# A two-layer conditioned trunk on one core: adaLN sums 1024 columns wide on VectorE, rope in three operations, wider splits and a new instruction list

## The chip, the core and the metric

The kernel runs on 1 core of one Trainium2 chip. The engines are TensorE (PE; its weight loads are listed apart as PEld), VectorE (DVE), ScalarE (ACT), GpSimd (POOL) and SyncE (SP, which issues most transfers). The metric is device time of one execution in microseconds (us), here the median of 3 runs. A profile is taken from one further execution of the same program.

## What is computed

Batch 1, 256 tokens, width 1024, two layers, fp32. Layer 0 is "even" (sliding-window heads A with sinks, beside heads B with compressed, selected and window keys), layer 1 is "odd" (16 heads, block attention).

```python
c_act = silu(c)
for layer in range(2):
    ada = c_act @ w_ada[layer] + b_ada[layer]      # 1024 -> 3 * 1024
    shift, scale, gate = split(ada, 3)
    h = rms_norm(x, norm_g[layer]) * (1 + scale) + shift
    y = even_mixer(h, ...) if layer == 0 else odd_mixer(h, ...)
    x = x + gate * y
return rms_norm(x, final_g)

def even_mixer(h):   # one input projection, two head groups, silu gate paths, one output projection
    oa = sliding_window(rope(q_a), rope(k_a), v_a, sinks) * silu(z_a)
    k_cmp, v_cmp = gelu((blocks + pe) @ w1) @ w2   # compressed keys and values: 15 blocks of 32 tokens
    ob = gates of (attention to k_cmp, to selected blocks, to a window) * silu(z_b)
    return concat(oa, ob) @ w_out
```

Shortened here; rope turns the two halves of each 64-wide head against each other: (x1 cos - x2 sin, x2 cos + x1 sin).

## The kernel before

Weights come from HBM once, as tiles `raw` of 128 x 2048 (a ring of `RAW` = 5). PE multiplies in a rounded form of fp32: a number is split into a rounded high half (`whi`, made by ACT) and the rest (`wlo`, a subtraction on DVE), and `mm3` makes three matmuls of the halves. `split` does so in pieces of `spl` columns; `SPL` holds that width for layer 0's attention, its out projection, and two parts of layer 1. The activations' halves are `hhi`, `hlo` (the input of a layer) and `ghi`, `glo` (the input of an out projection). Rings give `whi` and `wlo` four tiles each.

The adaLN sums c_act @ w_ada are, apart from layer 0's shift and scale (made in the start), cut into jobs that `fill()` puts between other work: layer 0's gate (`G0_ON`), layer 1's shift and scale (`SS_ON`) and layer 1's gate (`G1_ON`). Their letters say who does them. "v": DVE multiplies 512 columns of each of the eight row blocks by a scalar per partition and adds them up in `acc` (`ada_sums`, 8 pieces); then PE adds over the 128 partitions, by a matmul with ones. "p": PE does it all, by eight matmuls 32 x 256 that stand in four column groups (`ada_rows`, tiles `raw`, `cz`), a copy `asb`, and matmuls of `asb` with `selbc` or two columns of `ta`. The tile `cz` is silu(c).

Attention is done four softmaxes at a time (`attn_four`): scores on PE into `ps_s` (two banks), mask and maximum on DVE, exp on ACT, a division by multiplying with `rc` on DVE, or on ACT for the places in `ON_ACT` (a place is n, i, t; those with t = 1 are 256 wide), then transposes on PE. `compress` makes the compressed keys (`uT` is blocks + pe, `hx` and `hg` are the gelu's, `kcbd` the keys in block-diagonal form), and `cmp_softmax` their scores and softmax.

Every call on an engine is only recorded, by `Plan.record`; all instructions therefore carry the line of `Plan.issue`, which issues them (L251 here, L246 in the changed kernel). The order is the list `ORDER`, a permutation of the recorded calls, written out in the kernel. Each engine takes its own instructions strictly in that order; between engines only semaphores wait.

The jobs of layer 0 are spread so:

```python
jobs = [lambda: gate_bias(0)] + ada_jobs(ada_gate, 0, G0_ON, 2) + ada_jobs(ada_shift_scale, 1, SS_ON, 1)
spl[0] = SPL[0]
fill(1)
gate_path(W0, 640, 0); a_quad(0); ...; compress(); cmp_softmax(); fill(1); ...; b_pair(3, True); ...
spl[0] = SPL[1]
out_proj(w_out_even[0], lambda: fill(2))
fill(len(jobs))
```

Of the kernel before, what the change touches and what calls it, by code (L numbers as in the profile page):

```python
# [1356 lines left out]
```

## Time and profile before

| | |
|---|---|
| median of 3 runs | 307.33 us (306.77 to 308.2) |
| the profiled execution's own time | 307.55 us |
| its span | 305.4 us |
| instructions | 6362 |
| granted TensorE clock | 1.00 of full speed in every stretch from 71.6 to 298.2 us, 0.86 in the last 7 us |
| bytes read from HBM | 70.38 MB |

The span runs from the first to the last recorded instruction; the profiled execution's own time is 2.2 us more than that, and 0.2 us above the median. All times below are in us from the span's start unless a duration in ns is meant. A busy time is the time in which at least one instruction of the engine is in progress; matmuls overlap, so the durations of their records add up to more than the time PE spends on them. An fp32 matmul leaves two records in the trace, a rounded one leaves one.

Rough stages: the start, with layer 0's input projection, to 71.6; layer 0's attention to about 154; its out projection and the norm and input of layer 1 to about 163; layer 1 to 298.2, where PE ends; final norm and output to 305.4.

### The profile page before, as it was taken

The page shows a single profiled execution, that of the slowest core. Times are in us where ns is not written, and L with a number is a line of the kernel's source. Part 1 is how long each engine was busy: PE and PEld are TensorE (multiplying, and loading weights), DVE is VectorE, ACT ScalarE, POOL GpSimd, SP SyncE. Part 2 cuts the span into 40 slices and gives each one's busy share as a digit, 9 for nine tenths or more (in the row PEclk, how much of TensorE's full clock was granted, in tenths as well). Part 3 has the DMA queues.
Part 4 walks back from the last instruction along what each step waited for, and adds up shares of the span by engine and source line. Part 5 has one row for each costly group of instructions (what it writes and reads, how often), then busy time and mean ns, then how long its engine had stood idle before and what let it go on. Part 6 is the DMA issues. An engine that isn't in the chain of part 4 may idle for free.

```text
span 305.4 us, 6362 instructions
## 1 busy us (share of the span) xinstructions
PE 294.5 (96%) x2331; PEld 252.0 (83%) x2331; DVE 258.4 (85%) x703; ACT 184.3 (60%) x483; POOL 11.3 (4%) x36
## 2 busy tenths in 40 slices
PE   8899999999999999999999999999999999999990
PEld 8777788997789787888877899999789989877890
DVE  1388999998899999999989778598857999997783
ACT  3476147876679778882547854264647646873630
POOL 6000000002000000000001000000000000000011
PEclk9999999999999999999999999999999999999998
DMA  8999999986956979489899292968098493151003
GB/s 240 355 364 372 387 402 372 332 261 194 337 194 197 320 260 329 139 246 339 259 274 329 61 328 63 366 206 290 0 277 276 144 298 113 52 225 71 0 9 128
DMA packets 60669, 71.82 MB, mean 235 GB/s; under 512 B 2712, under 2 KB 52320, under 8 KB 60640
## 3 DMA queue, kind: packets, MB, share of 16 engines
q1 hardware_dynamic: 60032, 70.90, 70.1%
q10 hardware_dynamic: 448, 0.48, 0.4%
q8 instruction: 18, 0.29, 0.4%
q0 software_dynamic: 160, 0.05, 0.3%
q14 instruction: 11, 0.09, 0.1%
HBM read 70.38 MB, written 1.05 MB: 234 GB/s over the span
## 4 chain that ended last, share of the span: by engine, by line
PE 84%; ACT 4%; DMA 4%; DVE 3%; issue 2%; SPq 0%; POOL 0%; POOLq 0%; ACTq 0%; DVEq 0%
PE ps_pj L251 49%; PE ps_s L251 12%; PE ps_m L251 8%; PE ps_pt L251 7%; PE ps_o L251 7%; DMA raw<-in_w_in_even_dram 2%; DMA xs<-in_x_dram 2%; ACT whi L251 2%; DVE wlo L251 1%; ACT t L251 1%; DVE xs L251 1%; DVE t L251 1%; ACT bigA L251 1%; SPq L251 0%; ACT hhi L251 0%
## 5 line engine op out<-in xcount | busy, mean ns | idle before, releaser
L251 ACT CAST whi<-raw 128x512 fp32r<-128x512 f32 (+1 forms) x132 | 74.7, 599 | 28.8 <-PE ps_pj L251 17.2
L251 DVE TENSOR_TENSOR wlo<-raw,whi 128x512 fp32r<-128x512 f32 (+1 forms) x116 | 74.0, 659 | 8.9 <-ACT whi L251 8.7
L251 PE MATMUL ps_pj<-hhi,whi 128*128 128x256 f32 x256 | 68.0, 286 | 0.0
L251 PE MATMUL ps_pj<-hhi,wlo 128*128 128x256 f32 x256 | 67.8, 286 | 0.0
L251 PE MATMUL ps_pj<-hlo,whi 128*128 128x256 f32 x256 | 67.3, 283 | 0.0
L251 PEld LDWEIGHTS ps_pj<-hhi,whi 128*128 128x128 f32 x256 | 46.5, 188 | 1.1 <-issue 0.3
L251 PEld LDWEIGHTS ps_pj<-hhi,wlo 128*128 128x128 f32 x256 | 46.3, 188 | 0.6 <-issue 0.3
L251 PEld LDWEIGHTS ps_pj<-hlo,whi 128*128 128x128 f32 x256 | 46.3, 188 | 0.1
L251 DVE SCALAR_TENSOR_TENSOR acc<-raw,cz,acc 128x512 f32<-128x512 f32 x42 | 31.3, 745 | 0.3
L251 ACT ACTIVATE sm<-sm,mn 128x256 f32<-128x256 f32 (+1 forms) x58 | 26.0, 450 | 6.5 <-DVE mn L251 6.4
L251 PE MATMUL ps_pj<-whi,hhi 128*128 128x512 f32 (+2 forms) x72 | 26.0, 375 | 0.8 <-ACT hhi L251 0.8
L251 DVE SCALAR_TENSOR_TENSOR wlo<-raw,whi 128x512 fp32r<-128x512 f32 x32 | 21.2, 686 | 5.1 <-ACT whi L251 5.1
L251 PE MATMUL ps_pj<-wlo,hhi 128*128 128x512 f32 (+2 forms) x72 | 25.3, 377 | 0.0
L251 PE MATMUL ps_pj<-whi,hlo 128*128 128x512 f32 (+2 forms) x72 | 25.0, 369 | 0.0
L251 PE MATMUL ps_pj<-whi,ghi 128*128 128x512 f32 (+1 forms) x56 | 20.8, 375 | 0.0
L251 PE MATMUL ps_pj<-wlo,ghi 128*128 128x512 f32 (+1 forms) x56 | 20.5, 372 | 0.0
L251 ACT COPY pT<-ps_pt 128x384 f32<-128x384 f32 x25 | 11.9, 476 | 14.2 <-PE ps_pt L251 14.2
L251 PE MATMUL ps_pj<-whi,glo 128*128 128x512 f32 (+1 forms) x56 | 20.1, 365 | 0.0
L251 PEld LDWEIGHTS ps_pj<-whi,hhi 128*128 128x128 f32 x72 | 13.4, 188 | 3.5 <-ACT hhi L251 1.4
L251 PE MATMUL ps_pt<-ta,sm 128*128 128x128 f32 x87 | 15.7, 276 | 0.0
L251 DVE TENSOR_TENSOR t<-ps_pj,tb 128x512 f32<-128x512 f32 (+2 forms) x22 | 12.0, 586 | 3.4 <-PE ps_pj L251 3.4
L251 PEld LDWEIGHTS ps_pj<-wlo,hhi 128*128 128x128 f32 x72 | 13.3, 189 | 1.9 <-DVE wlo L251 0.2
(231 smaller groups left out, 613.2 us busy)
## 6 DMA issues: line engine op xcount, KB each, us to landing
raw<-in_w_in_odd_dram SPq DMA_DIRECT2D x16, 1024.0 KB, 7.6
raw<-in_w_ada_dram SPq DMA_DIRECT2D x28, 512.0 KB, 5.7
raw<-in_w_in_even_dram SPq DMA_DIRECT2D x8, 652.0 KB, 7.0
raw<-in_w_in_even_dram SPq DMA_DIRECT2D x5, 1024.0 KB, 9.0
t<-in_w_ada_dram SPq DMA_DIRECT2D x16, 256.0 KB, 6.0
raw<-in_w_out_even_dram SPq DMA_DIRECT2D x4, 1024.0 KB, 5.4
raw<-in_w_out_odd_dram SPq DMA_DIRECT2D x4, 1024.0 KB, 6.3
qT<-in_w_ada_dram SPq DMA_DIRECT2D x12, 256.0 KB, 7.2
```

The costliest lines, as they stand in the source:

```text
L251: self.ops.append(dict(key=eng.key, deps=deps, fn=lambda: getattr(real, name)(*args, **kw)))
```

## The change

1. The adaLN jobs are all done by DVE and are 1024 columns wide: `ada_wide` makes two multiply-adds of 1024 columns for each of four tiles `raw`. Layer 0's gate is one job, layer 1's shift and scale are two (four of the eight column blocks each, shift and scale together), layer 1's gate is one. Shift and scale end in four matmuls 32 x 256 in four column groups, a copy `asb` on ACT and two transposes. Layer 1's gate (`GATE_R`) splits its sums into rounded halves, and adds over the partitions by four rounded matmuls with ones in the place of two fp32 ones.
2. Rope: the two half-wide multiplications with the sine are one, which reads the halves of each head in reverse order by a negative step. `_box`, which finds which memory a call touches, learns negative steps.
3. `compress` adds the position rows in four additions instead of eight. `cmp_softmax` holds the compressed keys still and streams the queries, in four column groups, then copies and transposes back: 4 matmuls 32 x 256, one copy, 2 transposes for 8 matmuls of 128 x 32.
4. `SPL`: splits of 1024 columns in layer 0's attention and out projection.
5. `ON_ACT`: all the 256-wide scalings of `attn_four` (layer 0) go to ACT, twelve more than before.
6. The three sets of small rows share one transpose, `hr` has one buffer instead of two, and `ORDER` is a new list.

```diff
 START = ((2, 0), (2, 4), (2, 6), (2, 6))
-SS_ON = "vvvp"
-G0_ON = "vp"
-G1_ON = "vv"
-SPL = (512, 512, 512, 512)
+GATE_R = (0, 1)
+SPL = (1024, 1024, 512, 512)
 CUT = 384
-ON_ACT = ((0, 1, 1), (1, 1, 1))
+ON_ACT = ((0, 0, 1), (0, 1, 1), (1, 0, 1), (1, 1, 1))
 T4B = 4
 SMB = 5
 BANKS = {"pj": 3, "s": 2, "pt": 1, "o": 1, "m": 1}
@@ -35,131 +33,126 @@
 INIT = 3e38
...
 
         dims = [tuple(d) for d in ap.ap]
-        p0, f0 = divmod(ap.offset, dims[0][0])
+        off = ap.offset + sum(st * (n - 1) for st, n in dims[1:] if st < 0)
+        dims = dims[:1] + [(abs(st), n) for st, n in dims[1:]]
+        p0, f0 = divmod(off, dims[0][0])
         free = tuple(d for d in dims[1:] if d[0] and d[1] > 1)
...
-    rows = const([64, P], "rows")
-    rows_pe = const([32, P], "rows_pe")
+    rows = const([96, P], "rows")
...
-        T.transpose(pr[:, :64], rows, ident[:64, :64])
-        V.tensor_copy(rT[:, :64], pr[:, :64])
+        T.transpose(pr[:, :96], rows, ident[:96, :96])
+        V.tensor_copy(rT, pr[:, :96])
...
-    def ada_tile(l, cols, spare=None):
...
+    ones_r = const([P, P], "ones_r", F32R)
+    G.tensor_copy(ones_r, ones)
+    def ada_wide(l, c0, n, u, a):
         src = w_ada[l].rearrange("(k p) n -> p k n", p=P)
+        w = sb([P, 2048], "raw", RAW).rearrange("p (k n) -> p k n", n=1024)
+        for s in range(1024 // n):
+            Y.dma_start(w[:, :, s * n : s * n + n], src[:, 2 * u : 2 * u + 2, c0 + s * D : c0 + s * D + n])
+        for k in range(2):
+            ck = cz[:, 2 * u + k, 0:1]
+            if u == 0 and k == 0:
+                V.tensor_scalar(a, w[:, k, :], ck, None, op0=ALU.mult)
             else:
+                V.scalar_tensor_tensor(a, w[:, k, :], ck, a, op0=ALU.mult, op1=ALU.add)
+    def ada_shift_scale(l, g, a):
         pa = bank("m")
+        plan.group([
+            T.matmul(pa[32 * q : 32 * q + 32, : 2 * P], ones[:, 0:32], a[:, 256 * q : 256 * q + 256], start=True, stop=True, tile_position=(0, 32 * q))
+            for q in range(4)
+        ])
         asb = sb([P, 2 * P], "asb", 2)
         A.copy(asb, pa[:, : 2 * P])
+        pc = bank("m")
+        for b in range(2):
+            T.transpose(pc[:, b * P : (b + 1) * P], asb[:, b * P : (b + 1) * P], ident)
+        pv = pc[:, : 2 * P].rearrange("p (b s j e) -> p s j b e", b=2, s=2, j=2)[:, :, :, :, 0]
+        bs = bT[:, 24 * l : 24 * l + 16].rearrange("p (s j) -> p s j", s=2)[:, :, g : g + 4].rearrange("p s (j b) -> p s j b", b=2)
+        dst = shs[:, l, :, g : g + 4]
         for s in range(2):
+            V.tensor_tensor(dst[:, s].rearrange("p (j b) -> p j b", b=2), pv[:, s], bs[:, s], ALU.add)
+        V.tensor_tensor(dst[:, 1], dst[:, 1], ngT[:, 8 * l + g : 8 * l + g + 4], ALU.mult)
+    def ada_gate(l, a):
+        if GATE_R[l]:
+            hi, lo = split(a, 1024)
+        for h in range(2):
+            pc = bank("m")
+            hs = slice(512 * h, 512 * h + 512)
+            if GATE_R[l]:
+                T.matmul(pc, ones_r, hi[:, hs], start=True, stop=False)
+                T.matmul(pc, ones_r, lo[:, hs], start=False, stop=True)
             else:
+                T.matmul(pc, ones, a[:, hs], start=True, stop=True)
+            V.tensor_tensor(gate[:, hs], pc, gate[:, hs], ALU.add)
+    def ada_jobs(l, c0, n, fin):
+        a = sb([P, 1024], "acc", 1)
+        r = [lambda u=u: ada_wide(l, c0, n, u, a) for u in range(4)]
+        last = r.pop()
+        return r + [lambda: (last(), fin(a))]
...
         V.tensor_tensor(t1, src, cs.unsqueeze(1).to_broadcast([P, n, HD]), ALU.mult)
-        V.tensor_tensor(t2[:, :, 0:32], src[:, :, 32:64], sn[:, 0:32].unsqueeze(1).to_broadcast([P, n, 32]), ALU.mult)
-        V.tensor_tensor(t2[:, :, 32:64], src[:, :, 0:32], sn[:, 32:64].unsqueeze(1).to_broadcast([P, n, 32]), ALU.mult)
+        V.tensor_tensor(
+            t2.rearrange("p h (u d) -> p h u d", u=2),
+            src.rearrange("p h (u d) -> p h u d", u=2)[:, :, ::-1, :],
+            sn.rearrange("p (u d) -> p u d", u=2).unsqueeze(1).to_broadcast([P, n, 2, 32]),
+            ALU.mult,
+        )
         dst = t1 if dst is None else dst
...
     def start_sums(g, n, d, w):
-        a = sb([P, 512], "acc", 1)
+        a = sb([P, 1024], "acc", 1)
...
-                for g in range(2):
-                    V.tensor_tensor(
-                        uT[:, 8 * hf : 8 * hf + 8, g, 0:15],
-                        src[:, :, g, :],
-                        pe.unsqueeze(2).to_broadcast([P, 8, 15]),
-                        ALU.add,
-                    )
+                V.tensor_tensor(
+                    uT[:, 8 * hf : 8 * hf + 8, :, 0:15],
+                    src,
+                    pe.unsqueeze(2).unsqueeze(3).to_broadcast([P, 8, 2, 15]),
+                    ALU.add,
+                )
...
-            hr = sb([P, 2, 4, 32], "hr", 2)
+            hr = sb([P, 2, 4, 32], "hr", 1)
...
     def cmp_softmax():
+        pa = bank("m")
+        plan.group([
+            T.matmul(pa[32 * hp_ : 32 * hp_ + 32, :S], kcbd[:, hp_ // 2, :], qbT[:, hp_, :], start=True, stop=True, tile_position=(0, 32 * hp_))
+            for hp_ in range(4)
+        ])
+        asb = sb([P, 2 * P], "asb", 2)
+        A.copy(asb, pa[:, :S])
         pc = bank("m")
         for t in range(2):
-            for hp_ in range(4):
-                T.matmul(
-                    pc[:, t * P + 32 * hp_ : t * P + 32 * hp_ + 32],
-                    qbT[:, hp_, t * P : (t + 1) * P],
-                    kcbd[:, hp_ // 2, :],
-                    start=True,
-                    stop=True,
-                )
+            T.transpose(pc[:, t * P : (t + 1) * P], asb[:, t * P : (t + 1) * P], ident)
...
-    jobs = [lambda: gate_bias(0)] + ada_jobs(ada_gate, 0, G0_ON, 2) + ada_jobs(ada_shift_scale, 1, SS_ON, 1)
+    jobs = [lambda: gate_bias(0)] + ada_jobs(0, 2 * D, 1024, lambda a: ada_gate(0, a))
+    for g_ in (0, 4):
+        jobs += ada_jobs(1, P * g_, 512, lambda a, g_=g_: ada_shift_scale(1, g_, a))
...
-    jobs += ada_jobs(ada_gate, 1, G1_ON, 2)
+    jobs += ada_jobs(1, 2 * D, 1024, lambda a: ada_gate(1, a))
```

Where layer 0's attention does adaLN sums on DVE, its instructions stood so before (an ISA row is a mask with a maximum; `sm`, `bigA` softmax tiles, `den`, `rc` their sums and reciprocals, `mn` the maxima):

```order
L251 TENSOR_SCALAR sm_125<-sm_125,rc_138 128x128
L251 TENSOR_TENSOR wlo_114<-raw_101,whi_110 128x512
L251 TENSOR_SCALAR acc_105<-raw_100,cz 128x512
L251 SCALAR_TENSOR_TENSOR acc_105<-raw_100,cz,acc_105 128x512 x2
L251 ISA sm_124,mn_134<-ps_s_90,tb 128x128
L251 ISA mn_134 128x1
L251 ISA sm_125,mn_134<-ps_s_91,tb 128x256
L251 ISA mn_134 128x1
```

On the same engine at the same place of the program the new list has:

```order
L246 TENSOR_SCALAR sm_125<-sm_125,rc_137 128x128
L246 TENSOR_TENSOR wlo_113<-raw_100,whi_109 128x1024
L246 RECIPROCAL rc_138<-den_135 128x4
L246 TENSOR_TENSOR vz<-ps_m_66,blk 128x512
L246 SCALAR_TENSOR_TENSOR acc_104<-raw_101,cz,acc_104 128x1024
L246 ISA sm_124,mn_133<-ps_s_90,tb 128x256
L246 ISA mn_133 128x1
L246 SCALAR_TENSOR_TENSOR acc_104<-raw_101,cz,acc_104 128x1024
L246 ISA sm_124,mn_133<-ps_s_90,tb 128x128
```

Between the mask operations stand pieces of 1024 columns, a subtraction and two multiply-adds, where a subtraction, a first product and two multiply-adds of 512 stood.

On PE, at the border of the layers (`ghi`, `glo` are the out projection's input, `hhi`, `hlo` layer 1's; ta with `t` is a transpose of layer 1's input), before:

```order
L251 MATMUL ps_s_91<-whi_109,glo 128x512
L251 MATMUL ps_o_96<-ta,t_86 128x128
L251 MATMUL ps_m_67<-raw_102,cz 32x256 x8
L251 MATMUL ps_pj_92<-whi_110,hhi 128x512
L251 MATMUL ps_pj_92<-wlo_114,hhi 128x512
L251 MATMUL ps_pj_92<-whi_110,hlo 128x512
L251 MATMUL ps_pj_92<-whi_110,hhi 128x512
L251 MATMUL ps_pj_92<-wlo_114,hhi 128x512
L251 MATMUL ps_m_67<-ta,asb_107 128x2
```

and in the new list, from the last matmul of the out projection:

```order
L246 MATMUL ps_s_90<-whi_108,glo 128x512
L246 MATMUL ps_pj_93<-ta,t_85 128x128 x2
L246 MATMUL ps_o_95<-ta,t_85 128x128
L246 MATMUL ps_pj_93<-ta,t_85 128x128 x2
L246 MATMUL ps_pj_91<-whi_109,hhi 128x512
L246 MATMUL ps_pj_91<-wlo_113,hhi 128x512
L246 MATMUL ps_o_95<-ta,t_85 128x128
L246 MATMUL ps_pj_93<-ta,t_88 128x128 x4
L246 MATMUL ps_pj_91<-whi_109,hlo 128x512
L246 MATMUL ps_pj_91<-whi_109,hhi 128x512
L246 MATMUL ps_o_95<-ta,t_85 128x128 x2
```

The eight matmuls of the last "p" job no longer stand ahead of layer 1's first matmul, but more of the transposes of its input stand behind it. A little further on, the second shift-and-scale job of layer 1 ends among layer 1's matmuls:

```order
L246 MATMUL ps_pj_92<-whi_109,hlo 128x512
L246 MATMUL ps_m_66<-acc_104,ones 32x256 x4
L246 MATMUL ps_pj_92<-whi_110,hhi 128x512
L246 MATMUL ps_pj_92<-wlo_114,hhi 128x512
L246 MATMUL ps_m_66<-ta,asb_105 128x128 x2
```

Its four matmuls and two transposes stand where the two-column matmuls of `ta` and `asb` stood.

More of the change, by code (lines that the diff above doesn't have):

```diff
@@ L325, in tile_trunk @@
     G.dma_start(rows[0:16, :], norm_g.rearrange("l (k p) -> (l k) p", p=P))
-    G.dma_start(rows_pe[0:16, :], cmp_pe_k.rearrange("o (i t) d -> (o i) (t d)", t=2))
-    G.dma_start(rows_pe[16:32, :], cmp_pe_v.rearrange("o (i t) d -> (o i) (t d)", t=2))
+    G.dma_start(rows[64:80, :], cmp_pe_k.rearrange("o (i t) d -> (o i) (t d)", t=2))
+    G.dma_start(rows[80:96, :], cmp_pe_v.rearrange("o (i t) d -> (o i) (t d)", t=2))
     ident = ta[:, 0:128]
@@ L365, in small_rows @@
             V.tensor_scalar(bs, bs, 1.0, None, op0=ALU.add)
-        pr = bank("pt")
-        T.transpose(pr[:, :32], rows_pe, ident[:32, :32])
-        V.tensor_copy(rT[:, 64:96], pr[:, :32])
     oT = const([P, KT, S], "oT")
@@ L404, in tile_trunk @@
     glo = const([P, KT, S], "glo", F32R)
-    def ada_tile(l, cols, spare=None):
-        if spare is None:
-            raw = sb([P, 2048], "raw", RAW)
-            spare = (raw[:, :1024], raw[:, 1024:])
+    ones_r = const([P, P], "ones_r", F32R)
+    G.tensor_copy(ones_r, ones)
+    def ada_wide(l, c0, n, u, a):
         src = w_ada[l].rearrange("(k p) n -> p k n", p=P)
-        halves = []
-        for u in range(2):
-            w = spare[u].rearrange("p (k n) -> p k n", k=4)
-            ks = slice(4 * u, 4 * u + 4)
-            if cols[1] == cols[0] + 1:
-                Y.dma_start(w, src[:, ks, cols[0] * P : (cols[0] + 2) * P])
-            else:
-                for s in range(2):
-                    Y.dma_start(w[:, :, s * P : (s + 1) * P], src[:, ks, cols[s] * P : (cols[s] + 1) * P])
-            halves.append(w)
-        return halves
@@ L424, in ada_rows @@
-    def ada_rows(w):
-        pa = bank("m")
-        for i in range(2):
-            for q in range(4):
-                k = 4 * i + q
-                T.matmul(
-                    pa[32 * q : 32 * q + 32, : 2 * P],
-                    cz[:, k, :],
-                    w[k // 4][:, k % 4, :],
-                    start=(i == 0),
-                    stop=(i == 1),
-                    tile_position=(0, 32 * q),
-                )
+        w = sb([P, 2048], "raw", RAW).rearrange("p (k n) -> p k n", n=1024)
@@ L437, in ada_rows @@
         asb = sb([P, 2 * P], "asb", 2)
         A.copy(asb, pa[:, : 2 * P])
-        return asb
-    def ada_sums(l, cols, u, a):
-        src = w_ada[l].rearrange("(k p) n -> p k n", p=P)
-        w = sb([P, 2048], "raw", RAW).rearrange("p (k n) -> p k n", n=512)
-        for s in range(2):
-            Y.dma_start(w[:, :, s * 256 : s * 256 + 256], src[:, 4 * u : 4 * u + 4, cols[s] * P : (cols[s] + 2) * P])
-        for k in range(4):
-            ck = cz[:, 4 * u + k, 0:1]
-            wk = w[:, k, :]
-            if u == 0 and k == 0:
-                V.tensor_scalar(a, wk, ck, None, op0=ALU.mult)
-            else:
-                V.scalar_tensor_tensor(a, wk, ck, a, op0=ALU.mult, op1=ALU.add)
@@ L455, in ada_shift_scale @@
-    def ada_shift_scale(l, g, n, a=None, st=None):
-        gs = slice(g, g + n)
-        bview = bT[:, 24 * l : 24 * l + 16].rearrange("p (s j) -> p s j", s=2)[:, :, gs]
-        if a is None:
-            a = ada_rows(ada_tile(l, (g, 8 + g)))
-        st = st if st is not None else ones if n == 2 else sel
-        pc = bank("m")
-        for q in range(2 * n):
-            T.matmul(pc[:, 2 * q : 2 * q + 2], a[:, q * P : (q + 1) * P], st[:, 0:2], start=True, stop=True)
-        pv = pc[:, 0 : 4 * n].rearrange("p (s j e) -> p s j e", s=2, e=2)[:, :, :, 0]
-        ng = ngT[:, 8 * l + g : 8 * l + g + n]
-        V.tensor_tensor(shs[:, l, 0, gs], pv[:, 0, :], bview[:, 0, :], ALU.add)
-        if n == 1:
-            V.scalar_tensor_tensor(shs[:, l, 1, gs], pv[:, 1, :], bview[:, 1, :], ng, op0=ALU.add, op1=ALU.mult)
-        else:
-            V.tensor_tensor(shs[:, l, 1, gs], pv[:, 1, :], bview[:, 1, :], ALU.add)
-            V.tensor_tensor(shs[:, l, 1, gs], shs[:, l, 1, gs], ng, ALU.mult)
@@ L474, in tile_trunk @@
-    selbc = const([P, P], "selbc")
-    G.tensor_copy(selbc, sel[:, 0:1].to_broadcast([P, P]))
-    def ada_gate(l, h, n, a=None):
-        pc = bank("m")
-        if n == 2:
-            T.matmul(pc, ones, a, start=True, stop=True)
-        else:
-            T.matmul(pc[:, :256], selbc, ada_rows(ada_tile(l, (16 + h, 17 + h))), start=True, stop=True)
-        gs = gate[:, h * P : (h + 2 * n) * P]
-        V.tensor_tensor(gs, pc[:, : 256 * n], gs, ALU.add)
-    def ada_jobs(fn, l, on, w):
-        r = []
-        for i, ch in enumerate(on):
-            if ch == "v":
-                c0 = 2 * i * w
-                cols = (c0, 8 + c0) if fn is ada_shift_scale else (16 + c0, 18 + c0)
-                a = sb([P, 512], "acc", 1)
-                r.append(lambda cols=cols, a=a: ada_sums(l, cols, 0, a))
-                r.append(lambda cols=cols, a=a, c0=c0: (ada_sums(l, cols, 1, a), fn(l, c0, 2, a=a)))
-            else:
-                r += [lambda i=i, j=j: fn(l, (2 * i + j) * w, 1) for j in range(2)]
-        return r
+        pc = bank("m")
@@ L715, in start_sums @@
     def start_sums(g, n, d, w):
-        a = sb([P, 512], "acc", 1)
+        a = sb([P, 1024], "acc", 1)
         av = a[:, : 256 * n].rearrange("p (s c) -> p s c", s=2)
@@ L951, in cmp_softmax @@
     def cmp_softmax():
+        pa = bank("m")
[5 more added lines that the diff above has]
+        A.copy(asb, pa[:, :S])
         pc = bank("m")
         for t in range(2):
-            for hp_ in range(4):
-                T.matmul(
-                    pc[:, t * P + 32 * hp_ : t * P + 32 * hp_ + 32],
-                    qbT[:, hp_, t * P : (t + 1) * P],
-                    kcbd[:, hp_ // 2, :],
-                    start=True,
-                    stop=True,
-                )
+            T.transpose(pc[:, t * P : (t + 1) * P], asb[:, t * P : (t + 1) * P], ident)
         mcmp = tb[:, 1024:1056].rearrange("p (t b) -> p t b", t=2)
```

245 rows, old and new, of the table ORDER are left out of this document.

## The prediction

> **What bounds the kernel now.** I read the busy totals and the chain first, to see which engine ends the program; then the busy time by stretch, because a total is an average over stages; then, on VectorE (DVE), the idle gaps of the stretches where it is full; last the groups and single instructions that the change touches. The first two rows are from the page.
>
> ```profile
> PE 294.5 (96%) x2331; PEld 252.0 (83%) x2331; DVE 258.4 (85%) x703; ACT 184.3 (60%) x483; POOL 11.3 (4%) x36
> PE 84%; ACT 4%; DMA 4%; DVE 3%; issue 2%; SPq 0%; POOL 0%; POOLq 0%; ACTq 0%; DVEq 0%
> ```
>
> TensorE (PE) carries the chain, so a us off PE looks like a us off the time. The stretches say otherwise. Columns: window, its length, then busy us and count of PE, weight load, DVE, ACT, POOL, granted clock, DMA share, GB/s. Layer 0's attention starts at 71.6, its out projection ends near 163, layer 1 follows, PE ends at 298.2.
>
> ```profile
> 71.60:85.00 13.40, 13.18 (x134) 9.92 (x135) 11.49 (x56) 9.23 (x34) 0.62 (x2) 1.00 0.89 284
> 85.00:154.00 69.00, 69.00 (x553) 56.38 (x553) 68.19 (x220) 50.34 (x152) 0.00 (x0) 1.00 0.78 251
> 154.00:163.10 9.10, 9.10 (x57) 6.60 (x56) 7.85 (x21) 4.92 (x11) 0.94 (x3) 1.00 0.97 310
> 163.10:180.00 16.90, 16.90 (x104) 13.65 (x103) 14.45 (x33) 13.91 (x31) 0.67 (x1) 1.00 0.65 210
> 180.00:270.00 90.00, 90.00 (x797) 84.10 (x796) 75.78 (x202) 51.81 (x134) 0.00 (x0) 1.00 0.61 199
> 270.00:298.20 28.20, 28.20 (x169) 22.67 (x167) 23.16 (x43) 12.60 (x28) 1.59 (x4) 1.00 0.13 48
> 298.20:305.40 7.20, 0.24 (x3) 0.04 (x1) 2.57 (x7) 0.62 (x1) 0.67 (x1) 0.86 0.30 118
> ```
>
> From 85 to 154 two engines are full at once: PE 69.00 of 69, DVE 68.19. Over 71.6 to 163.1 (91.5 us) DVE is busy 11.49 + 68.19 + 7.85 = 87.5, so it idles 4.0 us: that is all that layer 0 can give while DVE keeps its work. In layer 1 only PE is full, so a us of PE there counts in full. Where DVE's idle lies outside the full stretch (start, busy us, operation, idle before it and its cause):
>
> ```profile
> 73.82 0.42 DVE L251 TENSOR_TENSOR t<-t 128x256 f32<-128x256 f32 x1
> 74.15 0.43 DVE L251 TENSOR_TENSOR t<-oT,tb 128x256 f32<-128x256 f32 x1
> 75.34 0.35 DVE L251 CUSTOM_DVE_ANT_0 sm<-ps_s,tb,snk 128x128 f32<-128x128 f32 x1 [0.76 <-PE ps_s L251]
> ...
> 81.08 0.23 DVE L251 COPY hx<-ps_m 128x64 f32<-128x64 f32 x1 [0.70 <-ACT sm L251]
> ...
> 82.38 0.23 DVE L251 SCALAR_TENSOR_TENSOR hg<-th,hx 128x64 f32<-128x64 f32 x1 [0.32 <-ACT th L251]
> ...
> 155.75 0.69 DVE L251 TENSOR_TENSOR t<-ps_s,gate 128x512 f32<-128x512 f32 x1 [0.62 <-PE ps_s L251]
> ...
> 158.51 0.22 DVE L251 SCALAR_TENSOR_TENSOR shs<-ps_m,rT 128x1 f32<-128x1 f32 x1 [0.43 <-PE ps_m L251]
> ...
> 163.11 0.43 DVE L251 TENSOR_TENSOR hlo<-t,hhi 128x256 fp32r<-128x256 f32 x1
> ```
>
> PE is the cause of 0.76 + 0.62 + 0.43 = 1.8 us of it; 163.11 is the first low half of layer 1's input.
>
> **What DVE's instructions cost.** On a full engine the price of an instruction is the distance to the next start, not its duration:
>
> ```profile
> 107.87 0.48 DVE L251 TENSOR_SCALAR acc<-raw,cz 128x512 f32<-128x512 f32 x1
> 108.27 0.42 DVE L251 CUSTOM_DVE_ANT_0 sm<-ps_s,tb 128x256 f32<-128x256 f32 x1
> ...
> 108.61 0.35 DVE L251 TENSOR_SCALAR sm<-sm,rc 128x256 f32<-128x256 f32 x1
> 108.87 0.28 DVE L251 CUSTOM_DVE_ANT_0 bigA<-ps_s,tb 128x128 f32<-128x128 f32 x1
> ...
> 109.08 0.69 DVE L251 TENSOR_TENSOR wlo<-raw,whi 128x512 fp32r<-128x512 f32 x1
> 109.69 0.75 DVE L251 SCALAR_TENSOR_TENSOR acc<-raw,cz,acc 128x512 f32<-128x512 f32 x1
> 110.35 0.68 DVE L251 SCALAR_TENSOR_TENSOR oT<-oT,ps_pj 128x512 f32<-128x512 f32 x1
> ```
>
> So 512 wide: first product 0.40, subtraction 0.61, multiply-add 0.66; a 256-wide scale by a scalar 0.26. Two 256-wide operations with two tensors are 0.33 apart (73.82, 74.15), so 256 more columns cost 0.28 and a start costs some 0.06 to 0.07. At 1024 I estimate, from these slopes, 1.14 for a subtraction, 1.20 for a multiply-add, and 0.66 for the first product (0.14 per 256 columns, from 0.26 and 0.40).
>
> ```profile
> L251 DVE SCALAR_TENSOR_TENSOR acc<-raw,cz,acc 128x512 f32<-128x512 f32 x42 | 31.3, 745 | 0.3
> L251 DVE TENSOR_SCALAR acc<-raw,cz 128x512 f32<-128x512 f32 x6 | 2.9, 478 | 0.0
> L251 DVE TENSOR_SCALAR sm<-sm,rc 128x256 f32<-128x256 f32 x20 | 6.8, 345 | 0.0
> L251 ACT ACTIVATE sm<-sm,rc 128x256 f32<-128x256 f32 x9 | 4.5, 505 | 2.7 <-DVE rc L251 2.7
> ```
>
> **The change on DVE, layer 0.**
> - adaLN sums: before, 4 jobs on DVE of 8 pieces of 512 columns (one for the gate, three for layer 1's shift and scale): 4 × (0.40 + 7 × 0.66) = 20.1. After, 3 jobs of 8 pieces of 1024: 3 × (0.66 + 7 × 1.20) = 27.2. **+7.1**.
> - Twelve 256-wide softmax scalings go to ACT: 12 × 0.26 = **−3.1**. ACT's price is at most 12 × 0.505 = 6.1 us; in the full stretch it is busy 50.34 of 69, so this is hidden, unless PE's transposes wait for one of them.
> - Merged pairs, each saving one start of 0.07: 16 splits (32 subtractions of 512 become 16 of 1024) −1.1, 8 rope calls −0.55, 4 compressed-key additions −0.3. Together **−1.95**. A rope with its halves reversed by a negative step has no row here: at best it saves its start, at worst the reversed operand streams at half rate, 256 columns for 0.28 more in each of the 8 calls, +2.2 instead of −0.55. I take −0.55, since the two operations that it replaces read the same columns, and keep the other end for the range.
> - Fewer small additions for shift, scale and gate (0.07 each): **−0.45**.
>
> Sum: 7.1 − 3.1 − 1.95 − 0.45 = **+1.6 us** of DVE work before layer 1.
>
> **The change on PE.**
>
> ```profile
> L251 PE MATMUL ps_m<-raw,cz 128*32 128x256 f32 x64 | 4.3, 385 | 0.0
> L251 PE MATMUL ps_m<-ones,acc 128*128 128x2 f32 x24 | 3.3, 212 | 0.0
> L251 PE MATMUL ps_m<-acc,ones 128*128 128x512 f32 x6 | 3.1, 592 | 0.0
> L251 PE MATMUL ps_m<-kcbd,qT 128*128 128x32 f32 x16 | 2.4, 233 | 0.0
> L251 PE MATMUL ps_m<-asb,selbc 128*128 128x256 f32 x4 | 1.2, 378 | 0.0
> L251 PE MATMUL ps_m<-ta,asb 128*128 128x2 f32 x8 | 1.1, 209 | 0.0
> ...
> 154.15 0.40 PE L251 MATMUL ps_s<-whi,ghi 128*128 128x512 f32 x1
> 154.38 0.40 PE L251 MATMUL ps_s<-wlo,ghi 128*128 128x512 f32 x1
> ...
> 155.64 1.07 PE L251 MATMUL ps_m<-raw,cz 128*32 128x256 f32 x16
> 156.64 0.50 PE L251 MATMUL ps_s<-whi,glo 128*128 128x512 f32 x1
> ...
> 163.34 1.08 PE L251 MATMUL ps_m<-raw,cz 128*32 128x256 f32 x16
> 164.34 0.50 PE L251 MATMUL ps_pj<-whi,hhi 128*128 128x512 f32 x1
> ```
>
> An fp32 matmul leaves two records. Start to start, the four PE jobs (raw, cz) take 1.0 us each, 4.0 in all; the two-column finishes 1.8 + 0.6, the compressed scores 1.3, the broadcast of the gate 0.9 by the same reading: 8.6 go. Added: three sets of four 32 × 256 matmuls at half a job each (1.5), six transposes at an estimated 0.11 (0.7), and half of layer 0's gate as one more fp32 matmul (0.9): net −5.5 in layer 0. In layer 1 the gate's two fp32 matmuls (four of the 592-ns records, 0.43 apart, 1.7) become four rounded ones at 0.23 (154.15 to 154.38): −0.8. But the new list puts one shift-and-scale finish behind layer 1's first matmul (+0.7, with −0.3 for the two-column matmuls that stood there) and three or four transposes of layer 1's input: I count layer 1's PE as **0**.
>
> What the −5.5 is worth in layer 0: DVE is full, so only DVE's waits on PE can go. I take the 1.8 named above, and half of the 0.81 us that DVE idles in the full stretch: **−2.2**. Against it stands DVE's **+1.6**. At the border PE, not DVE, ends last: the job at 163.34 stands between the last out-projection work and layer 1's first matmul at 164.34 and is now gone: **−1.0**. The first layer-1 matmul then waits for the ACT rounding and DVE subtraction of its input, 0.43 us, which its first term does not need.
>
> The rest costs nothing: same weight bytes with fewer transfers (128 issues become 116 on SP's queue), each needed no earlier; the start has no split that changes; the tail from 298.2 is the same 7.2 us. In layer 1 DVE does as much as before (gate sums 2 × 5.0 to 9.1, −0.9, and one subtraction for their rounded halves, +1.1), behind a full PE. A 1024-wide split reaches PE later by one more half of rounding and subtraction; the ring of four weight tiles covers it.
>
> Sum: −2.2 + 1.6 − 1.0 = −1.6. The profiled execution is 307.55, 0.2 above the median of 307.33; 307.55 − 1.6 = 305.9, **305.7** against the median.
>
> **Rivals.**
> - *Nothing measurable.* The idle does not go: the waits at 81.08 and 82.38 come from ACT, which now has twelve more scalings, and PE's finishes now wait for a copy and two transposes. Then +1.6 − 1.0 = +0.6: 307.9; with half of the idle gone 306.8.
> - *Slower.* A 1.2-us piece in place of a 0.66-us one stands ahead of score operations, and PE has only two banks for scores; each time PE runs out and DVE later waits back, 0.53 is lost. From the +0.6 above, two such losses pass the 0.5% line, four give +2.7, 310.0. Against it: 40 wide pieces, but PE has 5.5 us less to do. A rope at half rate (+2.7 against my sum) gives 308.4 alone, and slower with one loss more.
> - *More than forecast.* All 4.0 us of idle go, and the gate's −0.8 in layer 1 counts: −4.0 + 1.6 − 1.0 − 0.8 = −4.2, 303.1. The full PE saving, −6.3 and 301.0, needs a DVE that is not the bound, which 68.19 of 69 speaks against.
> - *Each start costs more.* If an instruction cost its whole duration, the sum on DVE would turn: sums 3 × (0.75 + 7 × 1.28) − 4 × (0.48 + 7 × 0.745) = +6.3, scalings −12 × 0.345 = −4.1, each of the 28 merges about 0.15, −4.2, and −0.45: −2.5 instead of +1.6, and the time near 301.6. The rows speak against it: the multiply-add at 109.69 lasts 0.75 and the next starts 0.66 later, the subtraction at 109.08 lasts 0.69 and is followed after 0.61. I give it 0.02. [...]
>
> **Chances.** Forecast 0.46 (own range 304.6 to 306.4; 0.36 of it under the line), nothing measurable 0.28, slower 0.16, more 0.10 (0.02 of it by the costlier starts). A measurement here can tell some 0.5% (1.5 us) from no change, so faster means below 305.8: 0.36 + 0.10 = 0.46; within 0.10 + 0.28 = 0.38; slower, above 308.9, 0.16. The range 303.0 to 309.0 leaves out the far ends of the last two cases.
>
> **What would show it.** In the changed profile: multiply-adds of 1024 about 1.28 us long and 1.2 apart; DVE over 98% busy from about 85 to 154 and PE no longer full there, with gaps put down to DVE; the idle before ps_s and shs gone; the first layer-1 matmul near 162.8; from there to PE's end the same 133.8 us. I am wrong if PE stays full in layer 0 (then DVE was not the bound), if the rope's merged operation takes over 0.5 us, or if PE waits for a split of 1024.

## The result, and the profile after

| | before | changed |
|---|---|---|
| median | 308.56 us (306.77 to 310.57, 20 runs) | 305.62 us (303.76 to 309.23, 20 runs) |
| ratio | | 0.9913 (0.989 to 0.9935) |

The kernel became 2.7 us faster (0.87%, interval 2.0 to 3.4 us); 305.7 had been forecast against the median of 307.33 then known, a gain of 1.6. Over twenty runs the kernel before came out 1.2 us higher than over those three, so the changed kernel's median lies at the forecast one although the gain is 1.1 us larger.

The page of the changed kernel's profiled execution first. That execution took 308.12, one of the slowest of the twenty, so the second execution below (e1, the same kernel, 305.57) is the one to compare by stage.

```profile
PE 290.3 (95%) x2246; PEld 246.3 (81%) x2246; DVE 257.8 (84%) x639; ACT 188.0 (61%) x479; POOL 12.0 (4%) x36
...
PEclk9989999999999999999997999999999999999998
...
PE 62%; DVE 20%; DMA 8%; issue 3%; SPq 3%; ACT 1%; POOL 1%; POOLq 0%; ACTq 0%; DVEq 0%
```

PE carried 84% of the chain before, now 62%, and DVE 20% instead of 3%. The clock row has a new dip in the middle. The stretches of that execution, columns as in the prediction:

```profile
12.00:16.00 4.00, 2.75 (x65) 2.40 (x66) 0.68 (x3) 0.16 (x2) 0.00 (x0) 0.79 1.05 404
16.00:20.00 4.00, 3.13 (x16) 2.57 (x17) 2.94 (x11) 3.87 (x10) 0.00 (x0) 0.79 0.85 288
...
85.00:154.00 69.00, 68.11 (x517) 52.93 (x517) 68.62 (x186) 56.18 (x157) 1.16 (x2) 1.00 0.80 279
154.00:163.10 9.10, 6.82 (x31) 5.08 (x30) 8.61 (x20) 4.37 (x10) 1.74 (x4) 1.00 0.81 262
163.10:180.00 16.90, 16.42 (x80) 12.23 (x79) 12.11 (x28) 11.87 (x29) 0.45 (x1) 0.90 0.57 188
180.00:270.00 90.00, 90.00 (x803) 84.74 (x803) 77.78 (x199) 53.03 (x134) 0.00 (x0) 1.00 0.61 204
```

Two things are in it. In the start PE waited 2.01 us for the first adaLN weights, and the clock was 0.79 from 12 to 20 us; this belongs to this execution (the clock of e1 is 1.00 there). At the border of the layers PE is busy 6.82 of 9.1 us, where it had been 9.10, and the clock behind is 0.90; a wait of 2.15 us and a lower clock behind it are in both profiles of the changed kernel. The same border in e1, on PE, and then the stretch behind it:

```profile
158.28 0.38 PE L246 MATMUL ps_pj<-ta,t 128*128 128x128 f32 x2
160.81 0.79 PE L246 MATMUL ps_pj<-whi,hhi 128*128 128x512 f32 x1 [2.15 <-ACT hhi L246]
```

```profile
160.80:164.20 3.40, 3.39 (x12) 2.49 (x12) 3.11 (x10) 2.06 (x5) 0.55 (x1) 0.51 0.02 8
```

PE waits 2.15 us for the rounded input of layer 1, and then runs 3.4 us at half clock (0.51): 1.7 us of matmul work lost. Layer 1's first matmul moved from 164.34 to 160.81, but PE's last from 298.17 to 296.48 only. The milestone that does follow the time is DVE's first low half of layer 1's input (`hlo`). With the compressed keys (`kcbd`) as the other end, two of DVE's instructions that both kernels have (before's row of `hlo`, at 163.11, stands in the prediction):

```profile
82.53 0.22 DVE L251 TENSOR_TENSOR kcbd<-ps_m,blk 128x64 f32<-128x64 f32 x1
...
298.17 0.28 PE L251 MATMUL ps_pj<-whi,glo 128*128 128x256 f32 x1
```

and in e1:

```profile
82.44 0.22 DVE L246 TENSOR_TENSOR kcbd<-ps_m,blk 128x64 f32<-128x64 f32 x1
...
161.99 0.42 DVE L246 TENSOR_TENSOR hlo<-t,hhi 128x256 fp32r<-128x256 f32 x1
...
296.48 0.27 PE L246 MATMUL ps_pj<-whi,glo 128*128 128x256 f32 x1
```

| us, one profile each | to kcbd | kcbd to hlo | hlo to PE's last | rest | span |
|---|---|---|---|---|---|
| before | 82.53 | 80.58 | 135.06 | 7.22 | 305.39 |
| changed, e1 | 82.44 | 79.55 | 134.49 | 6.93 | 303.41 |
| difference | −0.09 | −1.03 | −0.57 | −0.29 | −1.98 |

From the keys to the border DVE was busy 78.52 of 80.58 us before, and 78.67 of 79.55 in e1: the same work, and 1.18 us less idle. The interval repeats well: it is 79.55 in four profiles of the changed list (the first, e1, e11, e12), and 79.89 in a fifth (e5). In the stretch from 85 to 154 both engines are still nearly full in e1, PE 68.50 and DVE 68.91 of 69:

```profile
85.00:154.00 69.00, 68.50 (x511) 53.14 (x512) 68.91 (x181) 54.29 (x149) 0.00 (x0) 1.00 0.77 272
```

The instruction sizes came out as estimated (groups of the profiled execution: busy us, mean ns of one | idle before; then three single instructions of it):

```profile
L246 DVE SCALAR_TENSOR_TENSOR acc<-raw,cz,acc 128x1024 f32<-128x1024 f32 x28 | 35.8, 1277 | 0.0
...
L246 DVE TENSOR_TENSOR wlo<-raw,whi 128x1024 fp32r<-128x1024 f32 x16 | 19.5, 1217 | 0.0
...
L246 DVE TENSOR_TENSOR t<-oT,tb 128x256 f32<-128x256 f32 x4 | 1.6, 418 | 0.0
```

```profile
150.09 1.22 DVE L246 TENSOR_TENSOR wlo<-raw,whi 128x1024 fp32r<-128x1024 f32 x1
151.23 1.28 DVE L246 SCALAR_TENSOR_TENSOR acc<-raw,cz,acc 128x1024 f32<-128x1024 f32 x1
152.42 0.68 DVE L246 TENSOR_TENSOR t<-ps_pj,gate 128x512 f32<-128x512 f32 x1
```

A split of 1024 keeps DVE 1.14 us (150.09 to 151.23) and a multiply-add 1.19; 1.14 and 1.20 had been estimated. Two of the four products in the last row of the groups are the rope's with the halves reversed; the mean of the four is 418 ns for 256 columns, and it was 420 for the two that the kernel before has: the reversed halves cost nothing.

### The profile page after: what moved, and what is told of

Its sections match the earlier page's. It is cut to its first block, busy times and chain, and to the rows that moved or that the text cites. A ratio compares the mean times of both kernels' runs of the same rounds, so it can differ in the third digit from the quotient of the medians.

```text
span 306.0 us, 6068 instructions
## 1 busy us (share of the span) xinstructions
PE 290.3 (95%) x2246; PEld 246.3 (81%) x2246; DVE 257.8 (84%) x639; ACT 188.0 (61%) x479; POOL 12.0 (4%) x36
## 3 DMA queue, kind: packets, MB, share of 16 engines
HBM read 70.38 MB, written 1.05 MB: 233 GB/s over the span
## 4 chain that ended last, share of the span: by engine, by line
PE 62%; DVE 20%; DMA 8%; issue 3%; SPq 3%; ACT 1%; POOL 1%; POOLq 0%; ACTq 0%; DVEq 0%
PE ps_pj L246 44%; DVE acc L246 6%; PE ps_s L246 5%; DMA raw<-in_w_in_even_dram 5%; PE ps_pt L246 5%; PE ps_m L246 5%; DVE wlo L246 4%; PE ps_o L246 3%; SPq L246 3%; DVE t L246 3%; DMA qT<-in_w_ada_dram 2%; DVE sm L246 2%; DVE bigA L246 2%; DMA ta<-in_tbl_a_dram 1%; DVE oT L246 1%
## 5 line engine op out<-in xcount | busy, mean ns | idle before, releaser
L246 ACT CAST whi<-raw 128x512 fp32r<-128x512 f32 (+2 forms) x116 | 72.2, 657 | 31.7 <-PE ps_pj L246 18.8
L246 DVE TENSOR_TENSOR wlo<-raw,whi 128x512 fp32r<-128x512 f32 (+2 forms) x100 | 71.6, 740 | 3.4 <-ACT whi L246 3.3
L246 PE MATMUL ps_pj<-hhi,whi 128*128 128x256 f32 x256 | 67.0, 284 | 0.0
L246 PE MATMUL ps_pj<-hhi,wlo 128*128 128x256 f32 x256 | 66.6, 284 | 0.0
L246 PE MATMUL ps_pj<-hlo,whi 128*128 128x256 f32 x256 | 65.7, 283 | 0.0
L246 DVE SCALAR_TENSOR_TENSOR acc<-raw,cz,acc 128x1024 f32<-128x1024 f32 x28 | 35.8, 1277 | 0.0
L246 PE MATMUL ps_pj<-whi,hhi 128*128 128x512 f32 (+2 forms) x72 | 26.7, 382 | 2.4 <-ACT hhi L246 2.4
L246 PE MATMUL ps_pj<-wlo,hhi 128*128 128x512 f32 (+2 forms) x72 | 26.1, 379 | 0.0
L246 PE MATMUL ps_pj<-whi,ghi 128*128 128x512 f32 (+1 forms) x56 | 20.1, 370 | 0.0
L246 PE MATMUL ps_pj<-whi,glo 128*128 128x512 f32 (+1 forms) x56 | 20.1, 364 | 0.0
L246 ACT COPY asb<-ps_m 128x128 f32<-128x128 f32 (+1 forms) x7 | 2.2, 313 | 20.8 <-PE ps_m L246 20.8
L246 PEld LDWEIGHTS ps_pj<-whi,hlo 128*128 128x128 f32 x72 | 13.5, 193 | 1.4 <-DVE hlo L246 0.2
```

The costliest lines, as they stand in the source:

```text
L246: self.ops.append(dict(key=eng.key, deps=deps, fn=lambda: getattr(real, name)(*args, **kw)))
```

## The experiments

Theory A is the prediction's: DVE bounds layer 0 of the changed kernel, PE layer 1, and the gain is what PE used to hold up. The ratios are to the kernel before, run beside each (its medians: 308.54 for e1 to e4, 308.20 for e5 to e8, 308.78 for e9 to e12). In e4 and e7 to e10 parts of the adaLN sums are left out or not issued, so these kernels only serve to measure time.

| run | what | median us | ratio (interval) | kcbd to hlo | hlo to PE's last |
|---|---|---|---|---|---|
| e1 | changed, again | 306.06 | 0.9931 (0.9902 to 0.996) | 79.55 | 134.49 |
| e2 | changed, old `ON_ACT` | 308.96 | 1.0019 (0.9992 to 1.0046) | 82.47 | 134.93 |
| e3 | before, new `ON_ACT` | 309.86 | 1.0037 (1.001 to 1.0064) | 81.66 | 135.04 |
| e4 | changed, half the sums | 305.23 | 0.988 (0.9843 to 0.9916) | 79.14 | 135.01 |
| e5 | changed, gap filled | 304.97 | 0.9895 (0.9863 to 0.9927) | 79.89 | 133.66 |
| e6 | changed, border reordered | 308.05 | 0.9997 (0.9971 to 1.0023) | 78.58 | 137.15 |
| e7 | before, no p matmuls | 308.36 | 1.0006 (0.9976 to 1.0037) | 80.69 | 135.01 |
| e8 | before, last p job without its matmuls | 307.92 | 0.9993 (0.9967 to 1.002) | 80.60 | 135.00 |
| e9 | before, half the sums | 307.31 | 0.997 (0.994 to 1.0) | 80.55 | 135.09 |
| e10 | before, half the sums and no p matmuls | 306.62 | 0.9927 (0.99 to 0.9953) | 79.35 | 135.03 |
| e11 | changed, two fills | 305.67 | 0.9883 (0.9842 to 0.9925) | 79.55 | 133.76 |
| e12 | changed, small fill | 305.02 | 0.9877 (0.9834 to 0.9919) | 79.55 | 135.12 |

**e1.** No edit.

> The changed kernel, nothing edited, once more with a profile, because its profiled execution (308.1) was 2.5 us above its median. Theory A (VectorE bounds layer 0 of the changed kernel, TensorE bounds layer 1, and the gain is what TensorE used to hold up): 305.5 to 306, DVE over 98% busy from 85 to 160, the wait of about 2.2 us of TensorE for the first rounded input of layer 1 is there again, and the clock is lower behind it. Rival B (TensorE bounds throughout and the profiled execution was disturbed in the start alone): the same time, but no wait at the border of the layers.

The time and the wait are there, and so is the lower clock behind it; B's "no wait at the border" is out.

**e2.**

```diff
-ON_ACT = ((0, 0, 1), (0, 1, 1), (1, 0, 1), (1, 1, 1))
+ON_ACT = ((0, 1, 1), (1, 1, 1))
```

> The changed kernel with the old ON_ACT: twelve 256-wide scalings back on DVE, 12 x 0.26 = 3.1 us, same order of calls. Theory A: they all lie on the bound, 2.5 to 3.5 us slower than the changed kernel (308 to 309). Rival B (TensorE bounds layer 0): 0 to 0.5 us slower.

2.9 us above e1 in the medians, and 2.92 more between the milestones, for 3.1 us of DVE work, with DVE's idle there as before (0.91 us, 0.88 in e1): in the changed kernel DVE is the bound for added work, as A says.

**e3.** The opposite edit to the kernel before.

> The kernel before with only the new ON_ACT: DVE 3.1 us less in layer 0, TensorE the same. Theory A says of the kernel before that both engines are full there, so that relief of DVE alone gives little: 0 to 1 us faster than before. Rival C (the scalings moved to ACT are the whole gain): 2.5 to 3 us faster than before.

It became slower (by 0.1 to 0.6%), which neither expected. DVE did 2.2 us less between the milestones (76.34 busy) and idled 5.3 instead of 2.1 us, most of the difference at waits that the kernel before does not have:

```profile
93.45 0.16 DVE L251 TENSOR_TENSOR den<-den,es 128x4 f32<-128x4 f32 x1 [0.73 <-ACT bigA L251]
...
124.78 0.49 DVE L251 TENSOR_SCALAR acc<-raw,cz 128x512 f32<-128x512 f32 x1 [0.50 <-PE ps_m L251]
...
133.97 0.69 DVE L251 SCALAR_TENSOR_TENSOR oT<-oT,ps_pj 128x512 f32<-128x512 f32 x1 [0.88 <-ACT oT L251]
```

In two of the three, moved scalings stand in ACT's queue ahead of what DVE waits for. Ahead of the last one, on ACT:

```profile
131.30 0.91 ACT L251 ACTIVATE bigA<-bigA,rc 128x256 f32<-128x256 f32 x2
...
133.35 0.59 ACT L251 ACTIVATE oT<-ps_pj 128x512 f32<-128x512 f32 x1
```

ACT had room (50.34 of 69 us busy in the full stretch, 73%), and yet the move did not pay in the old list; in the new one it does (e2).

**e4.** (The comment is added here.)

```diff
-                V.scalar_tensor_tensor(a, w[:, k, :], ck, a, op0=ALU.mult, op1=ALU.add)
+                i = V.scalar_tensor_tensor(a, w[:, k, :], ck, a, op0=ALU.mult, op1=ALU.add)
+                if k == 1 and not (l == 1 and c0 == 2 * D):
+                    plan.skip.add(i)       # recorded, not issued
```

> The changed kernel with the second product of each pair left out in layer 0's three adaLN jobs, twelve multiply-adds of 1024, 12 x 1.2 = 14.4 us of DVE work less in layer 0 (so half of these sums is missing). Theory A: DVE stops being the bound and TensorE takes over; before, TensorE was busy 91.3 us of 71.6 to 163.1 and has 6.2 less to do ahead of layer 1, so the floor is about 85 us against some 90 now: 3 to 5 us faster than the changed kernel (301 to 302.5). Rival B: 0 to 0.5 us faster.

With DVE 12 us freer between the milestones (66.77 us busy for 78.67) these come 0.41 us closer, little more than the scatter of 0.34 between two profiles. The medians differ by 0.8 us, the ratios by 1.6 (their intervals overlap). A's 301 to 302.5 is out: PE is right behind DVE. It stays nearly full to 154 (68.14 of 69), and the wait at the border is the same 2.15 us.

```profile
85.00:154.00 69.00, 68.14 (x512) 52.96 (x511) 57.38 (x172) 54.92 (x151) 0.46 (x2) 1.00 0.79 276
```

```profile
160.95 0.50 PE L247 MATMUL ps_pj<-whi,hhi 128*128 128x512 f32 x1 [2.15 <-ACT hhi L247]
```

So A was replaced by H: from the keys to the border both engines are full, before and after, and relief of one alone is worth little. e7, e9 and e10 test this on the kernel before; in the changed kernel, relief of PE alone was not run.

**e7 and e8.** The `raw,cz` matmuls of all four p jobs, or of the last one, are recorded and not issued (comments added here):

```diff
+                if True:                   # e8: if plan.pj == 3
+                    plan.skip.add(j)       # j: the matmul of raw and cz
```

> The kernel before without the 32 matmuls of its four TensorE jobs (raw, cz; those adaLN sums are missing): 4.0 us less on TensorE, DVE the same. Theory A (DVE is as full as TensorE in layer 0, so only DVE's waits on TensorE and the job at the border can go): 2 to 3 us faster than before (305.5 to 306.5). Rival B (TensorE alone is the bound): 4 us faster (304.5).

> The kernel before without the eight matmuls of the last TensorE job alone, the one in front of layer 1's first matmul: 1.0 us less at that one place. The prediction's term: 1.0 us faster than before (307.5). Rival G (DVE's low half at 163.1 to 163.5, or the rounding on ACT, holds layer 1's first matmuls anyway): 0 to 0.4 us faster.

Neither moved the time beyond its interval (some 0.3% either way), and between the milestones both are within 0.11 us of before. For e7 both A and B are out; in e8 G holds. In e7 PE has gaps (67.79 of 69) and DVE is as full as before; DVE's wait for `ps_s` at the border stays, and the one for `shs` is replaced by one for `parts`, the norm's factor, from GpSimd:

```profile
85.00:154.00 69.00, 67.79 (x525) 55.83 (x524) 68.14 (x221) 51.27 (x154) 0.00 (x0) 1.00 0.79 255
```

```profile
156.87 0.69 DVE L253 TENSOR_TENSOR t<-ps_s,gate 128x512 f32<-128x512 f32 x1 [0.69 <-PE ps_s L253]
...
159.86 0.49 DVE L253 TENSOR_SCALAR t<-xs,parts 128x512 f32<-128x512 f32 x1 [0.54 <-POOL parts L253]
```

In e8 layer 1's first matmul comes 1.06 us earlier (163.28 for 164.34), and three us later PE stands still for what DVE has not made:

```profile
163.28 0.47 PE L253 MATMUL ps_pj<-whi,hhi 128*128 128x512 f32 x1
...
166.28 0.50 PE L253 MATMUL ps_pj<-whi,hlo 128*128 128x512 f32 x1 [0.67 <-DVE hlo L253]
```

Rival G: the gain at the first matmul is given back at `hlo`, the second one, which DVE makes at 165.80. In every kernel of the old list that was profiled, hlo to PE's last is 135.0 to 135.1.

**e9 and e10.** e9 leaves out every second multiply-add of layer 0's DVE jobs (`if k % 2`), e10 does this and e7's edit.

> The kernel before with every second multiply-add of layer 0's four DVE jobs left out (sixteen of 512, 16 x 0.66 = 10.6 us of DVE work; those adaLN sums are half missing), TensorE the same. Theory H (before, both engines are full from the compressed keys to the border, so relief of one is worth nothing): 0 to 1 us faster than before. Rival I (DVE alone bounds layer 0, since relief of TensorE gave nothing): 3 to 4 us faster, up to DVE's idle on TensorE.

> The kernel before with both reliefs at once: 10.6 us less on DVE and the 4.0 us of the four TensorE jobs' matmuls left out. Theory H: now the time falls, by 2.5 to 4 us (304 to 305.5), though each relief alone gave 0 to 1. Rival J (the border of the layers, a chain of norm, transposes and rounding, sets the time whatever the load): 0 to 1 us faster.

```profile
85.00:154.00 69.00, 69.00 (x552) 56.41 (x551) 58.68 (x203) 50.22 (x151) 0.00 (x0) 1.00 0.79 253
```

In e9 (the row above) DVE has 10 us of room and PE is full: kcbd to hlo 80.55 for 80.58; rival I's 3 to 4 us are out. By the ratios, e10 is 2.25 us faster than before (interval 1.4 to 3.1), where the reliefs apart gave 0.9 (0 to 1.9; the medians differ by 1.5) and −0.2 (−1.1 to 0.7). Between the milestones, where the two full engines stand, it is 1.23 us shorter, where they gave 0.03 and −0.11. H is right in kind, for neither relief alone moves the milestones and both do; but its 2.5 to 4 us are too large, and J is right about the rest: in e10 neither engine is the last any more at the border, where PE waits for the norm's result.

```profile
158.80 0.33 PE L253 MATMUL ps_pj<-ta,t 128*128 128x128 f32 x1 [1.02 <-DVE t L253]
```

**e5, e11, e12: the clock.** A transpose of layer 1's input is repeated sixteen times (e12: eight) behind the last transpose that stands before the gap; e11 also repeats a warm-up matmul four times in front of the first adaLN weights.

```diff
+            for f in self.attach.get(i, ()):
+                f()                        # in issue(), behind call i
...
+                if t == 0 and k == 4:
+                    plan.attach[last3] = [plan.ops[i]["fn"]] * 16
```

> The changed kernel with sixteen repeats of one transpose of layer 1's input (128 x 128, the same data to the same place, 0.11 us each, some 1.8 us of extra TensorE work) in the gap of 2.15 us at the border of the layers. Theory D (a gap of about 2 us on TensorE makes the clock fall to half for some 3 us behind it, which cost 1.6 us in each profile of the changed kernel): no stretch of lower clock behind the border, 1 to 1.6 us faster than the changed kernel (304.3 to 305). Rival E (the lower clock comes from something else): the same clock, and the same time or up to 0.3 us slower.

> The changed kernel with the sixteen repeated transposes at the border, and four more warm-up matmuls (about 1 us) where TensorE waits for the first adaLN weights at about 12 us; that wait was 0.95 to 2.0 us long in the profiles and the clock fell only behind the longest. Theory D: no lower clock in either place, 304.5 to 305 in the median and a narrower spread of the runs than the changed kernel's 303.8 to 309.2. Rival K (the start follows the transfers alone): the same median and spread as with the gap at the border filled alone.

> The changed kernel with eight repeats instead of sixteen: a gap of about 1.25 us stays at the border. Theory D with the gaps seen so far (1.6 us and less without a lower clock, 2.0 and more with one): clock 1.00 behind the border, 304.5 to 305.5. Rival L (any gap of a us lowers the clock there): a stretch at half clock as in the changed kernel, 305.5 to 306.

The window shown of e1 above, in e5:

```profile
160.80:164.20 3.40, 2.51 (x15) 1.87 (x15) 3.38 (x10) 2.42 (x6) 0.55 (x1) 1.00 0.04 13
```

and e12's two waits, and the five us from 160 on in it:

```profile
160.37 0.50 PE L247 MATMUL ps_pj<-whi,hhi 128*128 128x512 f32 x1 [1.28 <-ACT hhi L247]
...
161.69 1.12 PE L247 MATMUL ps_pj<-ta,t 128*128 128x128 f32 x4 [0.49 <-DVE t L247]
```

```profile
160.00:165.00 5.00, 4.14 (x14) 3.25 (x15) 4.71 (x13) 3.66 (x9) 0.55 (x1) 0.67 0.02 6
```

With sixteen repeats (waits of 0.40 and 0.49 us are left) the clock stays at 1.00, and from hlo to PE's last it is 133.66, 0.8 us less than e1 (e11: 133.76). With eight a gap of 1.28 us is left, with a second of 0.49 us 0.8 us behind it, and the clock falls as before (0.67 over 5 us is 1.65 us lost), 135.12, as L has it for the border. So D's cause, idle time of PE at the border, is shown in the profiles, and its bound by the gap's length is not: 1.28 us at the border lowered the clock, waits of 1.29 (e5), 1.44 (e2) and 1.60 us (e6) for the adaLN weights did not. In the medians e5, e11 and e12 do not stand apart (305.0 to 305.7, intervals overlap), nor do they from the changed kernel; e11's runs, 303.95 to 306.5, were no closer together than e5's, so nothing is shown for the start. e5 beats the kernel before by 1.05% (0.7 to 1.4); that it beats the changed kernel too is not shown.

**e6.** The first two scale-and-shift operations of layer 1's input go ahead of the second token half's gate product, addition and mean square on DVE, in `ORDER`, in part:

```diff
-1641 ... 1579 1587 1588 1590 1580 1589 1581 1591 ...
+1641 ... 1587 1588 1590 1589 1591 1579 1656 1580 1592 1581 ...
```

> The changed kernel with one change of its list: on DVE the first two scale-and-shift operations of layer 1's input go ahead of the second token half's gate product, its addition and its mean square. Theory D: the gap falls from 2.15 to about 1.1 us, the clock stays at 1.00, 2 to 2.8 us faster than the changed kernel (303 to 304). Rival F (the second token half, now 0.65 us later, is what TensorE waits for next): the gap falls but a second one follows, 0 to 1 us faster.

```profile
161.95 0.50 PE L127 MATMUL ps_pj<-whi,hhi 128*128 128x512 f32 x1 [1.32 <-ACT hhi L127]
...
164.94 0.66 PE L127 MATMUL ps_pj<-ta,t 128*128 128x128 f32 x4 [2.15 <-DVE t L127]
```

F, and worse than it said: the first gap shrank from 2.15 to 1.32, the transposes of the second half then waited 2.15, and the lower clock came behind that second wait:

```profile
162.00:165.00 3.00, 0.85 (x4) 0.45 (x4) 2.94 (x9) 1.54 (x3) 0.55 (x1) 1.00 0.06 19
165.00:168.50 3.50, 3.50 (x14) 2.85 (x15) 3.35 (x8) 2.52 (x7) 0.00 (x0) 0.63 0.00 0
```

It was 2 us slower than the changed kernel, by the ratios to the kernel before.

## Why the prediction was right, and where it was not

- **Both engines full, and no gain from PE's 5.5 us as such.** Right in the old list: e7 took 4.0 us off PE alone for nothing. But the prediction let DVE's idle of 1.8 us, put down to PE, go as a consequence of PE's relief; e7 shows that in the old list it does not go. In e1 DVE's waits for `ps_s` and `shs` are gone, as the prediction's signs have it, and DVE idles 1.18 us less between the milestones. Whether the new list alone does this, or PE's relief together with it, no run separates. The prediction also called itself wrong if PE stayed full in layer 0, and PE is still 68.50 of 69 us busy in e1: by e2 DVE is the bound for added work, by e4 PE is hardly less so.
- **The DVE sum, +1.6.** Mis-sized. The new, wide instructions cost what was said, but the old sums cost more: 0.66 was read where the next instruction does not need the result. Where two multiply-adds on the same `acc` follow each other, the second starts only after the first has ended. Before, and then in e1:

```profile
141.41 0.75 DVE L251 SCALAR_TENSOR_TENSOR acc<-raw,cz,acc 128x512 f32<-128x512 f32 x1
142.19 0.75 DVE L251 SCALAR_TENSOR_TENSOR acc<-raw,cz,acc 128x512 f32<-128x512 f32 x1
```

```profile
140.90 2.60 DVE L246 SCALAR_TENSOR_TENSOR acc<-raw,cz,acc 128x1024 f32<-128x1024 f32 x2
```

That is 0.78 from start to start instead of 0.66, and 1.32 (2.60 less one duration of 1.28) instead of 1.19. Counted by starts, layer 0's four jobs took 21.2 us before, not 20.1, and the three new ones 27.4 (forecast 27.2): 6.2 more, not 7.1. Over the whole program DVE's busy time fell from 258.4 to 257.9 us (e1), where the prediction's sums for both layers give +1.8. The sums explain 0.9 of these 2.3 us; the rest is not broken down. Where the work stands changes little. One multiply-add of the last job (1.2 us) and two splits of 512 (1.2) stand behind the first `hlo` in the new list, but the second token half's gate product, addition, mean square and scaling (2.3) now stand ahead of it. The gate product before, and then in e1:

```profile
163.45 0.68 DVE L251 TENSOR_TENSOR t<-ps_s,gate 128x512 f32<-128x512 f32 x1
```

```profile
158.34 0.68 DVE L246 TENSOR_TENSOR t<-ps_s,gate 128x512 f32<-128x512 f32 x1
```

Measured to the first `hlo`: 63.94 + 78.52 = 142.5 us busy before, 62.92 + 78.67 = 141.6 in e1, 0.9 less.
- **The job at the border, −1.0.** Wrong for the list from which it was read: e8 measured 0.0 from `hlo` to the end, since DVE's `hlo` holds layer 1 up. The prediction's sentence that the first term does not need `hlo` is true and beside the point; the third term does. For the new list it is not shown to be wrong. There the second token half's work is done before the first `hlo`, and behind the border PE does not run out any more; in e5:

```profile
163.10:180.00 16.90, 16.89 (x99) 13.13 (x99) 13.48 (x28) 12.36 (x29) 0.00 (x0) 1.00 0.57 188
```

The job stood at 163.34 to 164.34, behind the first `hlo` of before (163.11), so its 1.0 us is counted in the column from `hlo` to PE's last.
- **Layer 1, 0.** Mis-sized on both sides. With the clock kept the column from `hlo` on is 1.3 to 1.4 us shorter (e5, e11). By the rows, the largest part is the job just named, 1.0, and the next the gate's matmuls with ones, 1.7 us before and 1.2 in e5 by their starts (−0.8 forecast); no run shows these parts alone. A gap on PE that was not forecast, with half clock behind it, takes 0.8 of it back in e1, and all of it in the profile first shown (163.99 to 299.03, 135.04). So the first matmul of layer 1 came at 160.81 in e1, where about 162.8 was forecast, and from there to PE's end it took 135.7 us, not 133.8.
- **The rest, 0.** From PE's last matmul to the end it is 6.92 to 6.94 us in every profile of the changed kernel and its variants, and 7.09 to 7.22 with the old list; not explained.
- **ACT has room.** Right with the new list (e2: the twelve scalings are worth 2.9 us), wrong without it (e3).

That the forecast of 305.7 and the median of 305.62 agree is partly luck. The kernel before was slower than then known, the gain was 2.7 us for 1.6, and errors cancel in it: forecast were −0.6 to the border (−2.2 and +1.6) and −1.0 at it; measured in the profiles were −1.1 to `hlo`, −0.6 behind it up to PE's last, and −0.3 in the rest. Of the rivals, "starts cost more" is out as a rule: the next operation starts 1.14 us behind a split of 1.22. It holds in the rows above, where a multiply-add needs the result of the one in front of it (0.78 us from start to start for a duration of 0.75, 1.32 for 1.28). "Nothing measurable" had the right mechanism for the kernel before (e3, e7).
